# Row and column tiles of the array, and fewer but longer DVE instructions, in the state-space core of a decoder

## The chip, the cores and the metric

The program runs on one core of a Trainium2 chip. The metric is the device time of one execution in microseconds (us). Of the kernel before there are three timed runs: 1267.12, 1269.05 and 1270.66 us, median 1269.05 us.

## The reference, cut to what matters

The reference is a two-layer decoder on 512 tokens of 1024 channels. Layer 0 has a state-space mixer and a feed-forward part, layer 1 has attention and a feed-forward part. The change is in the mixer alone:

```
u = h @ w_in                                # 64 groups of 16 channels
bu = einsum('gnk,lgk->lgn', b, u)           # b complex: 64 states per group
x_l = a * x_(l-1) + bu_l                    # a complex and diagonal, scan over l
y = Re(einsum('gkn,lgn->lgk', c, x)) + d * u
z = gelu(y); val, gate = split(z @ w_glu); out = val * sigmoid(gate)
```

## The kernel before, in words

The 512 tokens are 128 chunks (C) of four places (T). The 64 groups are 32 pairs; eight channel tiles (NCT) take four pairs (PPC) each. A pair has 2 x 64 states, which fill the 128 partitions, and 2 x 16 channels. All operands of this core are float32.

`s5_core` first splits the input and the weights into two parts for the input projection (`project`, eight halves of 48 products of 256 columns, written here as lines L141 to L143), and works out powers of the transition (L315 to L386). Then each tile t goes through these steps:

- `coefs` (L437): the input weights `W` and output weights `E` for the four places, by products and sums on DVE and POOL (`g` is POOL). ACT copies `W` into the buffers `Wbd` and `W0`, and `spread` copies `E` into `Obd`: with zeros around them, so that the two groups of a pair stand in a block-diagonal operand of 128 rows.
- `rotor` (L498): cosine and sine of the chunk's rotation, `Cs` and `Sn`: four products on DVE, two sums on POOL.
- `taps` (L524, PE lines L532 and L535): the products within a chunk, evacuated by ACT into `Tb`.
- `turn_w` and `turn_u` (L547, L557): transposes of the input weights and of u.
- `scan` (L562): PE makes the chunk inputs V (L569), DVE rotates them (four products), POOL adds (`ra`, `rc`), DVE runs the recurrence over the 128 chunks (L581, eight scans of 128), rotates back (four products), and POOL adds the states `Xr`, `Xi`.
- `outputs` (L597 to L599): three products per pair, then GELU on ACT (L601).
- `turn_y` (L609): transposes back, and a split into two parts (`zh` on ACT, `zl` on DVE L157).
- `partial` (L623): each finished tile goes at once into the first output tiles of the gated unit (12 products of 512 columns).

The rest of the gated unit, the feed-forward parts and the attention follow. They are long runs of products of 512 columns, for which DVE and ACT split each weight slab (`wh`, `wl`, L129 and L130).

The order on every engine is set when the program is built: a scheduler moves the instructions by a cost model of its own (`TCARGS`). Each engine then works off its list in order, and waits on semaphores. Buffers with a name and `bufs=n` rotate over n places; four PSUM banks (`x`) rotate over all uses of the tile steps.

## Time and profile before

| | |
|---|---|
| timed runs, median | 1269.05 us |
| profiled execution: span, first to last instruction | 1265.5 us (the page gives no other time of it) |
| mixer core (first instruction to the last transposes of tile 7) | 0 to 229 us |
| rest of the gated unit, up to the first row sums of the feed-forward part | 229 to 310.6 us |
| PE, DVE, ACT and POOL busy in 0 to 229 us | 184.0, 203.8, 118.0, 151.8 us |

How to read it: PE is TensorE's products, DVE is VectorE, ACT ScalarE, POOL GpSimd. After 229 us PE has hardly a pause until the end of the program. Up to there every engine waits for some other in turn. The clock column is the share of TensorE's full clock that was granted: 1.00 is 2.4 GHz, 0.50 is 1.2 GHz. A PE row's duration overlaps the next one's: a row "x8" of 1.06 us whose single members last 0.275 us has its members (1.06 - 0.275) / 7 = 0.112 us apart. A float32 product stands as two records, a transpose as one.

### The profile page before, as it was taken

The page shows a single profiled execution, that of the slowest core. Times are in us where ns is not written, and L with a number is a line of the kernel's source. Part 1 is how long each engine was busy: PE and PEld are TensorE (multiplying, and loading weights), DVE is VectorE, ACT ScalarE, POOL GpSimd, SP SyncE. Part 2 cuts the span into 40 slices and gives each one's busy share as a digit, 9 for nine tenths or more (in the row PEclk, how much of TensorE's full clock was granted, in tenths as well). Part 3 has the DMA queues.
Part 4 walks back from the last instruction along what each step waited for, and adds up shares of the span by engine and source line. Part 5 has one row for each costly group of instructions (what it writes and reads, how often), then busy time and mean ns, then how long its engine had stood idle before and what let it go on. Part 6 is the DMA issues. An engine that isn't in the chain of part 4 may idle for free.

```text
span 1265.5 us, 15056 instructions
## 1 busy us (share of the span) xinstructions
PE 1207.8 (95%) x5808; PEld 1000.6 (79%) x5808; DVE 707.2 (56%) x1241; ACT 482.8 (38%) x815; POOL 276.6 (22%) x248
## 2 busy tenths in 40 slices
PE   5987878999999999999999899999999999999998
PEld 4987767788888888888878677777888888888887
DVE  9999988335744444433336877754664444443221
ACT  5475443324433322322224666653433223332210
POOL 4777765003000000000042544342200000000000
PEclk9997778999999999999999999999999999999999
DMA  4210001333223332333322111101333332223431
GB/s 158 80 30 21 18 9 37 97 100 99 95 92 99 100 100 91 94 103 92 94 82 81 36 36 41 50 1 51 100 100 100 100 100 92 93 95 100 118 121 49
DMA packets 31895, 99.82 MB, mean 79 GB/s; under 512 B 3664, under 2 KB 5712, under 8 KB 31824
## 3 DMA queue, kind: packets, MB, share of 16 engines
q1 hardware_dynamic: 31680, 98.86, 25.2%
q8 instruction: 45, 0.74, 0.2%
q14 instruction: 26, 0.21, 0.1%
q10 hardware_dynamic: 144, 0.00, 0.0%
HBM read 96.75 MB, written 2.10 MB: 78 GB/s over the span
## 4 chain that ended last, share of the span: by engine, by line
PE 78%; DVE 3%; ACT 1%; issue 0%; DMA 0%; POOL 0%; DVEq 0%; ACTq 0%
PE ps_ps L141 19%; PE ps_ps L142 19%; PE ps_ps L143 19%; PE ps_s L922 3%; PE ps_po L959 2%; PE ps_a L141 2%; PE ps_a L143 2%; PE ps_a L142 2%; PE ps_x L141 2%; PE ps_x L143 2%; PE ps_x L142 2%; PE ps_a L939 1%; PE ps_a L907 1%; DVE wl L130 1%; ACT wh L129 1%
## 5 line engine op out<-in xcount | busy, mean ns | idle before, releaser
L129 ACT ACTIVATE wh<-w 128x1024 fp32r<-128x1024 f32 (+3 forms) x193 | 190.7, 992 | 534.3 <-PE ps_ps L142 337.1
L130 DVE TENSOR_TENSOR wl<-w,wh 128x1024 fp32r<-128x1024 f32 (+3 forms) x193 | 230.7, 1197 | 201.6 <-ACT wh L129 201.5
L141 PE MATMUL ps_ps<-fh,wh 128*128 128x512 f32 x704 | 274.2, 390 | 0.0
L143 PE MATMUL ps_ps<-fh,wl 128*128 128x512 f32 x704 | 273.4, 389 | 0.0
L142 PE MATMUL ps_ps<-fl,wh 128*128 128x512 f32 x704 | 273.4, 389 | 0.0
L141 PEld LDWEIGHTS ps_ps<-fh,wh 128*128 128x128 f32 x704 | 132.2, 188 | 27.9 <-issue 0.5
L142 PEld LDWEIGHTS ps_ps<-fl,wh 128*128 128x128 f32 x704 | 132.2, 188 | 27.7 <-issue 0.5
L143 PEld LDWEIGHTS ps_ps<-fh,wl 128*128 128x128 f32 x704 | 132.2, 188 | 27.5
L141 PE MATMUL ps_ps<-ah,wh 128*128 128x512 f32 x352 | 136.9, 389 | 0.0
L142 PE MATMUL ps_ps<-al,wh 128*128 128x512 f32 x352 | 136.9, 389 | 0.0
L143 PE MATMUL ps_ps<-ah,wl 128*128 128x512 f32 x352 | 136.9, 389 | 0.0
L249 POOL TENSOR_TENSOR acc<-acc,sq 128x512 f32<-128x512 f32 x21 | 31.4, 1495 | 423.3 <-ACT sq L248 422.8
L698 DVE TENSOR_TENSOR ut<-ps_ps,rstd 128x512 f32<-128x512 f32 x44 | 30.4, 691 | 127.8 <-PE ps_ps L143 127.8
L143 PEld LDWEIGHTS ps_ps<-ah,wl 128*128 128x128 f32 x352 | 66.1, 188 | 13.8
L695 DVE TENSOR_TENSOR gt<-ps_ps,rstd 128x512 f32<-128x512 f32 x44 | 30.4, 691 | 83.2 <-PE ps_ps L143 83.1
L142 PEld LDWEIGHTS ps_ps<-al,wh 128*128 128x128 f32 x352 | 66.1, 188 | 13.7
L141 PEld LDWEIGHTS ps_ps<-ah,wh 128*128 128x128 f32 x352 | 66.1, 188 | 13.6
L930 POOL TENSOR_SCALAR p<-p,sm 128x128 f32<-128x128 f32 (+2 forms) x48 | 45.3, 948 | 64.4 <-DVE sm L928 54.2
L922 PE MATMUL ps_s<-kT,qT 96*128 96x256 f32 (+3 forms) x128 | 44.9, 454 | 1.8 <-ACT kT L909 1.0
L925 DVE TENSOR_REDUCE mx<-ps_s 128x1 f32<-128x128 f32 (+3 forms) x64 | 30.7, 487 | 22.2 <-PE ps_s L923 21.5
L927 ACT ACTIVATE p<-ps_s,mx 128x128 f32<-128x128 f32 (+3 forms) x64 | 33.3, 524 | 21.9 <-DVE mx L925 18.8
L156 ACT ACTIVATE ah<-ut 128x512 fp32r<-128x512 f32 x44 | 27.9, 633 | 30.8 <-DVE ut L699 30.8
(391 smaller groups left out, 2081.0 us busy)
## 6 DMA issues: line engine op xcount, KB each, us to landing
...
```

Source lines behind the costliest of these rows:

```text
L129: nc.scalar.activation(out=wh[:, c], in_=w[:, c], func=AF.Copy)
L130: nc.vector.tensor_tensor(out=wl[:, c], in0=w[:, c], in1=wh[:, c].bitcast(F32), op=ALU.subtract)
L141: nc.tensor.matmul(out=out, lhsT=lh, rhs=rh, start=start, stop=False)
L142: nc.tensor.matmul(out=out, lhsT=lh, rhs=rl, start=False, stop=False)
L143: nc.tensor.matmul(out=out, lhsT=ll, rhs=rh, start=False, stop=stop)
L249: nc.gpsimd.tensor_tensor(out=acc, in0=acc, in1=sq, op=ALU.add)
L695: v.tensor_tensor(out=gt, in0=pss[0], in1=rstd, op=ALU.mult)
L698: v.tensor_tensor(out=ut, in0=pss[1], in1=rstd, op=ALU.mult)
L922: nc.tensor.matmul(out=ps, lhsT=qT[:, i * P:n], rhs=kT[:, 0:n], start=True, stop=False)
L925: v.reduce_max(out=m1, in_=ps, axis=AX.X, negate=True)
L927: nc.scalar.activation(out=pb, in_=ps, func=AF.Exp, bias=m1, accum_out=s1)
L930: eng.tensor_scalar(out=pb, in0=pb, scalar1=s1, scalar2=None, op0=M_)
```

## The change

- The operands of 128 rows with zeros go (`Wbd`, `W0`, `Obd`). The products read one group at a time from 64 of the 128 rows, and write to 64 of the 128 columns where the output has 64 rows. `taps` becomes 32 products of 64 rows by 64 columns and two of 64 rows (two banks instead of one), `scan` 16 products of 64 by 64 with 128 moving columns (8 of 128 by 128 before), `outputs` four full products and 16 of 64 rows (12 full ones before). `turn_w` has four transposes instead of eight.
- `coefs` works out `W` and `E` for both real parts in three DVE instructions each, of 512 and of 640 elements; nothing of it is left on POOL. The signed copies of the powers that this needs (`ArS`, `AiN`, `GrS`, `GiS`) are made once, by eight ACT instructions.
- In `scan`, both sums of the rotations move from POOL to DVE, the eight scans of 128 become two of 512 (`RH` holds the decay, with a zero at each pair's first chunk, which ACT fills per tile), and the back rotation becomes two products of 1016.
- `rotor` has eight DVE products of 256 instead of four of 512; its two sums stay on POOL. Its `t1`, `t2` share the single buffers `pc`, `qc` with the scan's products.

```
-            sqs.append(cp.tile([P, S], F32, name="xsq", tag=("ra", "rb", "rc", "rd")[k % 4]))
+            if k % 2 == 0:
+                two = cp.tile([P, 2, S], F32, name="xsq", tag=("z", "z", "pc", "qc")[k // 2], bufs=2 if k < 4 else 1)
+            sqs.append(two[:, k % 2])
...
+        ArS, AiN, GrS, GiS = (sp.tile([P, NCT * 2, 2, 2 * n], F32, name=m) for m, n in (("ArS", T + 1), ("AiN", T + 1), ("GrS", T), ("GiS", T)))
+        for o, x, n, signs in ((ArS, Ar, T + 1, (1.0, -1.0)), (AiN, Ai, T + 1, (-1.0, -1.0)), (GrS, Gr, T, (1.0, 1.0)), (GiS, Gi, T, (-1.0, 1.0))):
+            for c in range(2):
+                nc.scalar.activation(out=o[:, :, c], in_=x.rearrange("p (a e) j -> p a (e j)", e=2), func=AF.Copy, scale=signs[c])
...
-        Wbd = [sp.tile([P, PPC, 2, T, 2, 16], F32, name=f"Wbd{i}") for i in range(NB)]
-        W0 = [sp.tile([P, PPC, 2, T, 2, 16], F32, name=f"W0{i}") for i in range(NB)]
-        Obd = [sp.tile([P, PPC, 2, T, 2, 16], F32, name=f"Obd{i}") for i in range(NB)]
-        Tb = [sp.tile([P, PPC, T, 2, 16], F32, name=f"Tb{i}") for i in range(3)]
-        Xr = [sp.tile([P, PPC, C], F32, name=f"Xr{i}") for i in range(NB)]
-        Xi = [sp.tile([P, PPC, C], F32, name=f"Xi{i}") for i in range(NB)]
+        Wz = [sp.tile([P, 2 * PPC, 5, 16], F32, name=f"Wz{i}") for i in range(NB)]
+        Tb = [sp.tile([P, 2, 2, 2, T, 16], F32, name=f"Tb{i}") for i in range(3)]
+        X = [sp.tile([P, 2, PPC, C], F32, name=f"X{i}") for i in range(NB)]
+        RH = [sp.tile([P, PPC, C], F32, name=f"RH{i}") for i in range(NB)]
...
+            g.memset(Wz[b], 0.0)
+            g.memset(X[b][:, :, :, 0:1], 0.0)
+            g.memset(RH[b][:, :, 0:1], 0.0)
...
+            def weigh(o, j, n, re, im):
+                def bb(x):
+                    return x.unsqueeze(2).broadcast_to([P, 2 * PPC, n, 16])
+
+                def gg(x):
+                    return x[:, 2 * t:2 * t + 2].rearrange("p a c (e j) -> p (a c e) j", e=2).unsqueeze(3).broadcast_to([P, 2 * PPC, n, 16])
+
+                ma, mb = (cp.tile([P, 2 * PPC, n, 16], F32, name="w" + z, tag="e" + z, bufs=1) for z in "ab")
+                tt(ma, bb(bc[:, j]), gg(re), M_)
+                tt(mb, bb(bc[:, j + 1]), gg(im), M_)
+                tt(o, ma, mb, A_)
+
+            W = cp.tile([P, 2 * PPC, T, 16], F32, name="W")
+            weigh(W, 0, T, GrS, GiS)
+            nc.scalar.activation(out=Wz[t % NB][:, :, 1:5:2], in_=W[:, :, 0:1, :].broadcast_to([P, 2 * PPC, 2, 16]), func=AF.Copy)
+            E = cp.tile([P, 2 * PPC, T + 1, 16], F32, name="E", bufs=3)
+            weigh(E, 2, T + 1, ArS, AiN)
+            coef[t] = {"E": E, "W": W}
...
+            t1 = cp.tile([P, PPC, C], F32, name="t1", tag="pc", bufs=1)
+            t2 = cp.tile([P, PPC, C], F32, name="t2", tag="qc", bufs=1)
...
             for o, x, y in ((Cs, bcs, bcs), (t1, bsn, bsn), (Sn, bsn, bcs), (t2, bcs, bsn)):
-                tt(o.rearrange("p a (b c) -> p a b c", b=8), lo16(x), hi16(y), M_)
+                for e in range(2):
+                    tt(o[:, 2 * e:2 * e + 2].rearrange("p a (b c) -> p a b c", b=8), pairs(x, e)[:, :, 0:16].unsqueeze(2).broadcast_to([P, 2, 8, 16]),
+                       pairs(y, e)[:, :, 16:24].unsqueeze(3).broadcast_to([P, 2, 8, 16]), M_)
             tt(Cs, Cs, t1, S_, g)
             tt(Sn, Sn, t2, A_, g)
...
+        def taps(t):
+
+
+            b = t % NB
+            E = coef[t]["E"]
+            kps = [self.ps("x") for _ in range(2)]
+            for odd in (1, 0):
+                for q in range(2):
+                    for c in range(2):
+                        for e in range(2):
+                            for g2 in range(2):
+                                h = slice(64 * g2, 64 * g2 + 64)
+                                r = 4 * q + 2 * c + e
+                                wz = Wz[b][h, r, (0 if odd else 1):(4 if odd else 5)]
+                                nc.tensor.matmul(out=kps[g2][64 * e:64 * e + 64, 64 * q + (0 if odd else 16):64 * q + 64],
+                                                 lhsT=wz.rearrange("p i k -> p (i k)"),
+                                                 rhs=E[h, r, 0:(T if odd else T - 1)].rearrange("p a b -> p (a b)"),
+                                                 start=odd == 1 and q == 0 and c == 0, stop=odd == 0 and c == 1, skip_group_check=True)
             for g2 in range(2):
                 h = slice(64 * g2, 64 * g2 + 64)
-                for c in range(2):
-                    nc.scalar.activation(out=Obd[t % NB][h, :, c, :, g2, :], in_=coef[t]["E"][h, :, c, 1:, :], func=AF.Copy)
-
...
-            for i in range(T):
-                r = slice(32 * i, 32 * i + 32)
-                for g2 in range(2):
-                    nc.scalar.activation(out=Tb[t % 3][r, :, T - 1 - i:, g2, :], in_=k4[r, :, 0:i + 1, :], func=AF.Copy,
-                                         scale=self.c("g2mask")[r, g2:g2 + 1])
+                nc.tensor.matmul(out=kps[g2][:, 0:128].rearrange("p (a u k) -> p a u k", a=2, u=T)[:, :, 0:2, :], lhsT=self.c("places")[h],
+                                 rhs=DI[h, 2 * t:2 * t + 2].rearrange("p a (u k) -> p a u k", u=2), start=False, stop=True, skip_group_check=True)
+            for g2 in range(2):
+                k4 = kps[g2][:, 0:128].rearrange("p (a u k) -> p a u k", a=2, u=T)
...
+            ps_w = self.ps("x")
+            W = coef[t]["W"].rearrange("p (a e) i k -> p a (e i k)", e=2)
+            for r in range(4):
+                nc.tensor.transpose(out=ps_w[:, r * P:(r + 1) * P], in_=W[:, r], identity=ident)
+            WT = cp.tile([P, 2, 2, P], F32, name="WT")
+            nc.scalar.activation(out=WT.rearrange("p a b c -> p (a b c)"), in_=ps_w, func=AF.Copy)
...
         def scan(t):
+
...
-            V = []
+            nc.scalar.activation(out=RH[b][:, :, 1:].rearrange("p (e a) c -> p e a c", e=2),
+                                 in_=rho[:, t * PPC:(t + 1) * PPC].rearrange("p (a e) -> p e a", e=2).unsqueeze(3).broadcast_to([P, 2, 2, C - 1]), func=AF.Copy)
+            ps_v = [self.ps("x") for _ in range(2)]
+            for q in range(2):
+                for c in range(2):
+                    for g2 in range(2):
+                        for e in range(2):
+                            h = slice(64 * e, 64 * e + 64)
+                            nc.tensor.matmul(out=ps_v[e][64 * g2:64 * g2 + 64, (2 * q + c) * C:(2 * q + c + 1) * C],
+                                             lhsT=WT[h, q, c, 64 * g2:64 * g2 + 64], rhs=uT[h, q, g2], start=True, stop=True)
+            pc, qc = (cp.tile([P, 2, PPC, C], F32, name=n, bufs=1) for n in ("pc", "qc"))
+            for e in range(2):
+                vv = ps_v[e].rearrange("p (a c k) -> p c a k", a=2, c=2)
+                for o, w in ((pc, Cs), (qc, Sn)):
+                    tt(o[:, :, 2 * e:2 * e + 2], vv, w[:, 2 * e:2 * e + 2].unsqueeze(1).broadcast_to([P, 2, 2, C]), M_)
+            z = cp.tile([P, 2, PPC, C], F32, name="z")
+            tt(z[:, 0], pc[:, 0], qc[:, 1], A_)
+            tt(z[:, 1], pc[:, 1], qc[:, 0], S_)
             for c in range(2):
...
-            tt(ra, V[0], Cs, M_)
-            tt(rd, V[0], Sn, M_)
-            tt(rb, V[1], Sn, M_)
-            tt(rc, V[1], Cs, M_)
-            tt(ra, ra, rb, A_, g)
-            tt(rc, rc, rd, S_, g)
-            for z in (ra, rc):
-                for pp in range(PPC):
-                    rj = rho[:, t * PPC + pp:t * PPC + pp + 1].broadcast_to([P, C])
-                    v.tensor_tensor_scan(out=z[:, pp], data0=rj, data1=z[:, pp], initial=0.0, op0=M_, op1=A_)
+                v.tensor_tensor_scan(out=z[:, c].rearrange("p a b -> p (a b)"), data0=RH[b].rearrange("p a b -> p (a b)"),
+                                     data1=z[:, c].rearrange("p a b -> p (a b)"), initial=0.0, op0=M_, op1=A_)
...
-            tt(xr, ra[:, :, :n], Cs[:, :, :n], M_)
-            tt(xi, ra[:, :, :n], Sn[:, :, :n], M_)
-            tt(rb[:, :, :n], rc[:, :, :n], Sn[:, :, :n], M_)
-            tt(rd[:, :, :n], rc[:, :, :n], Cs[:, :, :n], M_)
-            tt(xr, xr, rb[:, :, :n], S_, g)
-            tt(xi, xi, rd[:, :, :n], A_, g)
+            xc, xs = (cp.tile([P, 2, PPC, C], F32, name="x" + m, tag=m, bufs=1) for m in ("pc", "qc"))
+            for o, w in ((xc, Cs), (xs, Sn)):
+                tt(o[:, :, :, :n], z[:, :, :, :n], w[:, :, :n].unsqueeze(1).broadcast_to([P, 2, PPC, n]), M_)
+            tt(X[b][:, 0, :, 1:], xc[:, 0, :, :n], xs[:, 1, :, :n], S_)
+            tt(X[b][:, 1, :, 1:], xc[:, 1, :, :n], xs[:, 0, :, :n], A_)
 
...
+            uT, E = states[t], coef[t]["E"]
+            ps_y = [self.ps("x") for _ in range(2)]
+            for g2 in range(2):
+                for q in range(2):
+                    nc.tensor.matmul(out=ps_y[g2][:, 128 * q:128 * q + 128], lhsT=uT[:, q, g2], rhs=Tb[t % 3][:, q, g2].rearrange("p e j k -> p (e j k)"),
+                                     start=q == 0, stop=False, skip_group_check=True)
+            for q in range(2):
+                for e in range(2):
+                    for c in range(2):
+                        for g2 in range(2):
+                            h = slice(64 * g2, 64 * g2 + 64)
+                            nc.tensor.matmul(out=ps_y[g2][:, 128 * q + 64 * e:128 * q + 64 * e + 64], lhsT=X[b][h, c, 2 * e + q],
+                                             rhs=E[h, 4 * q + 2 * c + e, 1:].rearrange("p j k -> p (j k)"),
+                                             start=False, stop=c == 1, skip_group_check=True)
+            Y = cp.tile([P, T, PPC, 2, 16], F32, name="Y", bufs=1)
+            for g2 in range(2):
+                nc.scalar.activation(out=Y.rearrange("p j a b k -> p a j b k")[:, :, :, g2], in_=ps_y[g2][:, 0:256].rearrange("p (a j k) -> p a j k", a=PPC, j=T),
+                                     func=AF.Gelu_apprx_tanh)
...
         for t in range(NCT):
             for f, d in ((turn_u, 1), (later_u, 0), (rotor, 1), (scan, 1), (turn_w, 2), (later_p, 6), (outputs, 0),
-                         (taps, 2), (later_p, 7), (partial, -1), (turn_y, 0), (spread, 2), (coefs, 3)):
+                         (taps, 2), (later_p, 7), (partial, -1), (turn_y, 0), (coefs, 3)):
```

On PE, the first tile's steps, from its transposes of u (`ps_x<-ctab,U`) through the taps (`E` with the input weights `W` or `Wz`, and the skip weights `DI`) to the transposes of the weights. Before:

```order
L557 MATMUL ps_x<-ctab,U 128x128 x4
L532 MATMUL ps_x<-E,W_308 128x64
L535 MATMUL ps_x<-DI,ctab 128x16
L532 MATMUL ps_x<-E,W_308 128x64 x2
L535 MATMUL ps_x<-DI,ctab 128x16
L532 MATMUL ps_x<-E,W_308 128x64 x2
L535 MATMUL ps_x<-DI,ctab 128x16
L532 MATMUL ps_x<-E,W_308 128x64 x2
L535 MATMUL ps_x<-DI,ctab 128x16
L532 MATMUL ps_x<-E,W_308 128x64
L547 MATMUL ps_x<-ctab,Wbd_306 128x128 x8
```

And now:

```order
L544 MATMUL ps_x<-ctab,U 128x128 x4
L514 MATMUL ps_x<-E,Wz_314 64x64 x16
L514 MATMUL ps_x<-E,Wz_314 64x48 x16
L520 MATMUL ps_x<-DI,ctab 128x2x32 x2
L534 MATMUL ps_x<-ctab,W 128x128 x4
```

The skip weights no longer stand between the taps, the taps are 32 narrower products instead of eight, and the weight transposes are four instead of eight.

On DVE, the scan of tile 1 and what stands beside it (`ra`, `rc` are its two parts, `Xr`, `Xi` the states, `E` an output weight, `Cs`, `Sn` the rotor). Before, from its recurrence on:

```order
L581 SCALAR_TENSOR_TENSOR ra<-dr,ra 128x128 x4
L581 SCALAR_TENSOR_TENSOR rc<-dr,rc 128x128 x4
L320 TENSOR_TENSOR Xr_316<-ra,Cs 128x4x127
L320 TENSOR_TENSOR Xi_318<-ra,Sn 128x4x127
L320 TENSOR_TENSOR rb<-rc,Sn 128x4x127
L320 TENSOR_TENSOR rd<-rc,Cs 128x4x127
L320 TENSOR_TENSOR E<-ea,eb 128x4x80
L476 SCALAR_TENSOR_TENSOR E<-ea,eb 128x4x80
L320 TENSOR_TENSOR Sn<-bsn,bcs 128x512
L320 TENSOR_TENSOR ra<-ps_x,Cs 128x512
L320 TENSOR_TENSOR rd<-ps_x,Sn 128x512
```

And now, from the rotor on that this scan uses (`t` its products, `pc`, `qc` the products from PSUM, `z` both parts, `xpc`, `xqc` the back rotation):

```order
L322 TENSOR_TENSOR Cs<-bcs 128x256 x2
L322 TENSOR_TENSOR X_319<-xpc,xqc 128x4x127 x2
L322 TENSOR_TENSOR Sn<-bsn,bcs 128x256 x2
L322 TENSOR_TENSOR t_924<-bsn 128x256 x2
L322 TENSOR_TENSOR t_925<-bcs,bsn 128x256 x2
L322 TENSOR_TENSOR pc<-ps_x,Cs 128x2x256 x2
L322 TENSOR_TENSOR qc<-ps_x,Sn 128x2x256 x2
L322 TENSOR_TENSOR z<-pc,qc 128x512 x2
L571 SCALAR_TENSOR_TENSOR z<-RH_322,z 128x512 x2
L322 TENSOR_TENSOR xpc<-z,Cs 128x8x127
```

Eight short scans are two long ones, the sums into `z` stand here, and `pc` comes straight behind the rotor's `t`, whose buffer it takes.

On POOL, the stretch that serves one tile. Before (`wb`, `W`, `eb` belong to the weights, `ra`, `rc`, `Xr`, `Xi` to the scan, `Cs`, `Sn` to the rotor):

```order
L320 TENSOR_TENSOR Cs<-Cs,t_1190 128x512
L320 TENSOR_TENSOR ra<-ra,rb 128x512
L320 TENSOR_TENSOR rc<-rc,rd 128x512
L320 TENSOR_TENSOR Sn<-Sn,t_1191 128x512
L320 TENSOR_TENSOR Xr_316<-Xr_316,rb 128x4x127
L320 TENSOR_TENSOR Xi_318<-Xi_318,rd 128x4x127
L320 TENSOR_TENSOR wb<-bc,Gi 128x256 x2
L320 TENSOR_TENSOR Cs<-Cs,t_1354 128x512
L320 TENSOR_TENSOR W<-wa,wb 128x4x64 x2
L320 TENSOR_TENSOR ra<-ra,rb 128x512
L320 TENSOR_TENSOR rc<-rc,rd 128x512
```

And now, from the last step of the powers (`Gi`) on:

```order
L322 TENSOR_TENSOR Gi<-mm 128x128
L322 TENSOR_TENSOR Cs<-Cs,t_671 128x512
L322 TENSOR_TENSOR Sn<-Sn,t_672 128x512
L322 TENSOR_TENSOR Cs<-Cs,t_924 128x512
L322 TENSOR_TENSOR Sn<-Sn,t_925 128x512
```

Only the two rotor sums of each tile are left on POOL.

## Rows read from the trace of the kernel before

**Rows 1.** The page: busy time by engine and its share of the span.

```profile
PE 1207.8 (95%) x5808; PEld 1000.6 (79%) x5808; DVE 707.2 (56%) x1241; ACT 482.8 (38%) x815; POOL 276.6 (22%) x248
```

**Rows 2.** Busy time of each engine by stage, granted clock (PEclk), DMA share.

```profile
28.00:90.00 62.00, 61.56 (x473) 60.50 (x472) 59.33 (x115) 36.87 (x75) 45.94 (x46) 0.97 0.18 56
90.00:100.00 10.00, 0.97 (x5) 0.78 (x4) 10.00 (x12) 2.41 (x4) 6.74 (x7) 0.74 0.05 13
100.00:205.00 105.00, 88.57 (x505) 79.96 (x504) 96.86 (x146) 52.98 (x118) 75.39 (x53) 0.80 0.06 18
229.00:311.00 82.00, 81.22 (x356) 66.48 (x356) 36.37 (x41) 31.48 (x42) 9.64 (x7) 1.00 0.32 98
72.67:217.61 144.94, 117.95 (x720) 106.80 (x718) 133.53 (x198) 73.24 (x157) 100.17 (x74) 0.84 0.08 22
```

**Rows 3.** Groups of DVE by form, 72 to 218 us.

```profile
L581 DVE TENSOR_TENSOR_SCAN ra<-dr,ra 128x128 f32<-128x128 f32 x32 | 26.4, 881 | 1.4 <-POOL ra L320 1.4
L581 DVE TENSOR_TENSOR_SCAN rc<-dr,rc 128x128 f32<-128x128 f32 x32 | 11.2, 412 | 0.0
...
L320 DVE TENSOR_TENSOR rb<-ps_x,Sn 128x512 f32<-128x512 f32 x8 | 5.4, 681 | 2.1 <-PE ps_x L569 2.1
```

**Rows 4.** Groups of POOL by form, 72 to 218 us.

```profile
L320 POOL TENSOR_TENSOR Sn<-Sn,t 128x512 f32<-128x512 f32 x7 | 10.5, 1505 | 5.9 <-DVE t L320 5.9
...
L320 POOL TENSOR_TENSOR Cs<-Cs,t 128x512 f32<-128x512 f32 x7 | 9.4, 1341 | 2.8 <-DVE t L320 2.8
```

**Rows 5.** DVE in order of time: start, length, instruction, count, idle before.

```profile
110.34 0.68 DVE L320 TENSOR_TENSOR rd<-rc,Cs 128x508 f32<-128x508 f32 x1
110.93 0.48 DVE L320 TENSOR_TENSOR E<-ea,eb 128x320 f32<-128x320 f32 x1
...
131.26 0.42 DVE L320 TENSOR_TENSOR wa<-bc,Gr 128x256 f32<-128x256 f32 x1
131.59 0.49 DVE L476 SCALAR_TENSOR_TENSOR E<-ea,eb 128x320 f32<-128x320 f32 x1
```

**Rows 6.** DVE, the first product of tile 0 and the last of tile 7.

```profile
72.67 0.69 DVE L320 TENSOR_TENSOR ra<-ps_x,Cs 128x512 f32<-128x512 f32 x1
...
216.93 0.68 DVE L320 TENSOR_TENSOR rd<-rc,Cs 128x508 f32<-128x508 f32 x1
```

**Rows 7.** PE in order of time: taps (L532, L535), projection, inputs of a scan.

```profile
121.54 0.39 PE L535 MATMUL ps_x<-DI,ctab 32*128 32x16 f32 x2
121.86 0.66 PE L532 MATMUL ps_x<-E,W 128*128 128x64 f32 x4
122.45 0.39 PE L535 MATMUL ps_x<-DI,ctab 32*128 32x16 f32 x2
...
125.31 0.39 PE L142 MATMUL ps_g<-zl,wh 128*128 128x512 f32 x1
125.54 0.39 PE L143 MATMUL ps_g<-zh,wl 128*128 128x512 f32 x1
125.99 1.16 PE L569 MATMUL ps_x<-uT,WT 128*128 128x128 f32 x8
```

**Rows 8.** Durations of one product (ns, min/median/max), 128 rows and 32 rows.

```profile
L569 PE MATMUL ps_x<-uT,WT x128: 270/275/421, 71.6 to 207.8; 128*128 128x128 f32 x128
...
L801 PE MATMUL ps_s<-ctab,krraw x4: 221/222/243, 688.4 to 688.6; 32*128 32x32 f32 x4
```

**Rows 9.** PE, four transposes of 32 rows, in a later stage.

```profile
688.35 0.43 PE L801 MATMUL ps_s<-ctab,krraw 32*128 32x32 f32 x4
```

**Rows 10.** PE at the first outputs.

```profile
89.59 0.60 PE L557 MATMUL ps_x<-ctab,U 128*128 128x128 f32 x4
99.23 0.80 PE L597 MATMUL ps_x<-Tb,uT 128*128 128x128 f32 x2 [9.03 <-DVE rd L320]
```

**Rows 11.** PE, the last transposes of the core.

```profile
228.38 0.60 PE L609 MATMUL ps_x<-ctab,Y 128*128 128x128 f32 x4
```

**Rows 12.** The chain that ended last, where the feed-forward takes its first row sums.

```profile
310.58 0.86 PE ps_ps L689 x2
```

More of the change, by code (lines that the diff above doesn't have):

```diff
@@ new lines, in taps @@
+            for g2 in range(2):
[5 more added lines that the diff above has]
+                for e in range(2):
+                    for ip in range(2):
+                        h = slice(64 * e + 32 * ip, 64 * e + 32 * ip + 32)
+                        n = 2 * ip + 2
+                        nc.scalar.activation(out=Tb[t % 3][h, :, g2, e, T - n:, :], in_=k4[h, :, 0:n, :], func=AF.Copy)
@@ L555, in turn_u @@
             ps_u = self.ps("x")
-            for pp in range(PPC):
-                nc.tensor.transpose(out=ps_u[:, pp * C:(pp + 1) * C],
-                                    in_=Us[t // 2][:, (t % 2) * PPC + pp].rearrange("p a b c -> p (a b c)"), identity=ident)
-            nc.scalar.activation(out=uT.rearrange("p a b -> p (a b)"), in_=ps_u, func=AF.Copy)
+            U = Us[t // 2].rearrange("p (a e) i k -> p a (e i k)", e=2)
+            for r in range(4):
+                nc.tensor.transpose(out=ps_u[:, r * C:(r + 1) * C], in_=U[:, 4 * (t % 2) + r], identity=ident)
@@ L560, in turn_u @@
+            nc.scalar.activation(out=uT.rearrange("p a b c -> p (a b c)"), in_=ps_u, func=AF.Copy)
             states[t] = uT
@@ L564, in scan @@
             Sn, Cs, WT, uT = coef[t]["Sn"], coef[t]["Cs"], coef[t]["WT"], states[t]
-            V = []
-            for c in range(2):
-                ps_v = self.ps("x")
-                for pp in range(PPC):
-                    nc.tensor.matmul(out=ps_v[:, pp * C:(pp + 1) * C], lhsT=WT[c][:, pp], rhs=uT[:, pp], start=True, stop=True)
-                V.append(ps_v.rearrange("p (a b) -> p a b", a=PPC))
-            ra, rb, rc, rd = (cp.tile([P, PPC, C], F32, name=n) for n in ("ra", "rb", "rc", "rd"))
@@ L591, in outputs @@
+            tt(X[b][:, 0, :, 1:], xc[:, 0, :, :n], xs[:, 1, :, :n], S_)
+            tt(X[b][:, 1, :, 1:], xc[:, 1, :, :n], xs[:, 0, :, :n], A_)
         def outputs(t):
             b = t % NB
-            uT = states[t]
-            ps_y = self.ps("x")
-            for pp in range(PPC):
-                o = ps_y[:, pp * P:(pp + 1) * P]
-                nc.tensor.matmul(out=o, lhsT=uT[:, pp], rhs=Tb[t % 3][:, pp].rearrange("p a b c -> p (a b c)"), start=True, stop=False)
-                nc.tensor.matmul(out=o, lhsT=Xr[b][:, pp], rhs=Obd[b][:, pp, 0].rearrange("p a b c -> p (a b c)"), start=False, stop=False)
-                nc.tensor.matmul(out=o, lhsT=Xi[b][:, pp], rhs=Obd[b][:, pp, 1].rearrange("p a b c -> p (a b c)"), start=False, stop=True)
@@ L603, in outputs @@
+            Y = cp.tile([P, T, PPC, 2, 16], F32, name="Y", bufs=1)
+            for g2 in range(2):
+                nc.scalar.activation(out=Y.rearrange("p j a b k -> p a j b k")[:, :, :, g2], in_=ps_y[g2][:, 0:256].rearrange("p (a j k) -> p a j k", a=PPC, j=T),
+                                     func=AF.Gelu_apprx_tanh)
             states[t] = Y
```

108 lines of the change are left out of this document (22 added, 86 removed).

## The prediction, made before the changed kernel ran

> **What bounds the kernel now.** I read the page first: PE is busy 1207.8 of the span of 1265.5 us [rows 1], so nearly all of its 58 idle us must lie somewhere, and only a stage where PE waits can give time. The table by stage [rows 2] says where. From 28 to 90 us PE is busy 61.56 of 62 us at a granted clock of 0.97: saturated by the input projection. From 90 to 100 it works 0.97 of 10 us. From 100 to 205 it works 88.57 of 105 us at a granted clock of 0.80, while DVE works 96.86. From 229 on it is dense again (81.22 of 82 at 1.00), up to the first row sums of the feed-forward part at 310.58 [rows 12]. So the core is bounded by PE up to 90 us, by DVE from its first rotation product to its last, and by PE behind that.
>
> The first outputs show the handover: PE ends the transposes of u at about 90.2 and stands 9.03 us for DVE's `rd` [rows 10]. DVE's stretch runs from 72.67 to 217.61 (216.93 and 0.68) [rows 6], 144.94 us, of which it is busy 133.53 and idle 11.41 [rows 2].
>
> How much of the 133.53 is work? Where POOL is quiet, DVE instructions start 0.59 us apart after 508 elements and 0.33 after 256 [rows 5]. That is 0.066 us for each instruction and 1.03 ns for each element: 0.60 for 512, 0.40 for 320, 0.73 for 640, 1.12 for 1016 or 1024. The scans of `rc` take 11.2 us for 32, or 0.35 each; those of `ra`, the same instruction while POOL still adds, 881 ns in the mean against 412 [rows 3]. The order has 197 DVE instructions in this stretch: 72 of 512 (43.2), 32 of 508 (18.9), 20 of 320 (8.0), 8 of 256 (2.6), one of 1024 (1.1), 64 scans (22.4). Sum 96.3 us. So 37.2 us of DVE's busy time are disturbance, while POOL is busy 100.17 us [rows 2]: 0.37 us lost for each us of POOL.
>
> **The change part by part.** I follow DVE through the same stretch, then add what stands ahead of it and behind it.
>
> *DVE's own work.* The order now has 189 instructions from the first product of tile 0 to the last sum into `X` of tile 7: 73 of 512 (43.8), 52 of 256 (17.2), 15 of 640 (11.0), 16 of 508 (9.4), 17 of 1016 or 1024 (19.0) and 16 scans of 512. No scan of 512 is in the trace. At most it costs four of 128 (1.40), at least a product of 512 (0.60); the row it is nearest to is the scan, less three times the fixed 0.066, so I take 1.20, 19.2 in all. Sum 119.6 us: 23.3 more than now. The merging saves little; the sums taken over from POOL cost 16 x 0.60 + 16 x 0.59 = 19.0, and the coefficients about 1.7 more for each of five tiles.
>
> *Disturbance.* Of some sixteen POOL instructions per tile two remain, 14 in the stretch; `Sn` takes 1505 ns in the mean and `Cs` 1341 [rows 4], so 7 x 2.85 = 19.9 us of POOL. At 0.37 this costs 7.4 us. The bounds are nothing, and their full length, 19.9. I take 7.4 since the operations and their neighbours are the same as now. The Trainium skill, SBUF — State Buffer, section Who interferes with whom, says that a DVE instruction with two inputs in SBUF and a POOL instruction that reads SBUF lock each other out for a whole instruction. The slow scans of `ra` bear the lock out; by its letter the 14 sums could cost 19.9 and not 7.4, and that is a rival below.
>
> *Waits.* Of DVE's 11.4 idle us the waits for POOL's sums and for free buffers go. The wait for PE's inputs of the scan stays, 2.1 us in `rb`'s group [rows 3]. One is new: `t1` and `t2` share single buffers with the scan's `pc` and `qc`, so the first product of a scan waits until POOL has read `t1` and `t2`. In five of seven tiles the order has other work between; in two, as in tile 1, `pc` stands right behind the last rotor product `t`, and of POOL's sum behind that (1.5) I give it 0.8, the half. Behind the waiting `pc` stands the whole scan and, on PE, that tile's outputs. So 2.1 + 1.6 = 3.7 us; bounds nothing and 11.4. DVE's stretch becomes 119.6 + 7.4 + 3.7 = 130.7 us against 144.94.
>
> *The start.* DVE's first product waits for PE, which is saturated there, so each added PE record counts. The order puts 6 more projection products ahead of the first scan (0.7 us at 0.12, half of the 0.23 that 512 columns take [rows 7]). It puts 46 more records of the taps there: 35 narrow products and two for places, two records each, against 12, less four transposes. And all 32 records of the scan must be done where the first 8 sufficed. A narrow record is not in the trace. Eight full ones take 1.16 us with 0.275 for the last, so 0.126 apart there; the four of 32 rows and 32 columns take 0.43 with 0.222, so 0.07 apart [rows 7 to 9]. I take 0.07, the row nearest in size, and keep a quarter of that and 0.126 as ends. Taps 46 x 0.07 = 3.2 (0.8 to 5.8), scan 32 x 0.07 - 8 x 0.126 = 1.2 (nothing to 3.0). First product at 72.67 + 0.7 + 3.2 + 1.2 = 77.8; between 74 and 82. The Trainium skill, TensorE: Matmul & The Clock Gate, Part 3 (Packing small matmuls), says that products in different row groups run together, which these pairs could do. No row of this kernel shows it; by it a record would count about half and the start fall by 2.2 us, which is inside my bounds.
>
> *Around it.* The signed copies (eight ACT instructions, once) and the longer way from POOL's last power `Gi` over ACT to DVE lie beside the projection, where PE is the bound; if that cover were gone, they would cost about 2 us. ACT works 52.98 of 105 us [rows 2] and loses the copies into `Wbd`, `W0`, `Obd`: it is no bound.
>
> *The end.* DVE ends at 77.8 + 130.7 = 208.5 instead of 217.61, and POOL's last `Xr`, `Xi`, which came behind, are gone. Then the order has the last 32 records and products of outputs(7) (2.7), 20 products of the gated unit at 0.23 (4.6, GELU beside them), `turn_y` (0.7) and 366 more products before the first row sums, where before it has 353 (228.38 + 0.7 + 353 x 0.231 = 310.6 checks with [rows 11, 12]). 366 x 0.231 = 84.5. Row sums at 208.5 + 2.7 + 4.6 + 0.7 + 84.5 = 301.0 against 310.58: 9.6 us earlier. PE is dense behind that, so it is passed on whole. The profiled span of 1265.5 becomes 1255.9. The median of the timed runs is 3.5 above this span (the page gives no other time), so the median 1269.05 becomes 1259.5, rounded to 1260.
>
> **Does PE keep up?** Per tile it gets 128 narrow records (9.0 at 0.07), 12 full ones (1.5), 12 transposes (1.3), 12 products of 512 columns (2.8), and about ten changes between narrow and full operands. Such a change costs: from one `L535` pair to the next, 121.54 to 122.45, lie four full records and two narrow ones, 4 x 0.126 + 2 x 0.07 = 0.64 of 0.91, so about 0.13 for each of two [rows 7]. Sum 15.9 us at full clock. DVE needs for a middle tile coefficients 4.0, rotor 2.7, scan and rotations 9.4, parts of slabs and of the output 1.2, together 17.3, and with disturbance 1.1 and waits 0.5 it is 18.9. So DVE stays the bound, but at the granted clock of 0.80 of this stretch PE would need 19.9: the margin is thin.
>
> **The rivals.**
> - *PE and DVE wait for each other.* At a clock of 0.80 PE loses 1.0 us on DVE in each of five middle tiles, and with both lists in order I put 4 more us of waits to it: 9 in all, 1269. For it: 0.80 now [rows 2], and PE works as much as before. Against: where PE has no gaps, the clock is 0.97 to 1.00.
> - *The narrow records cost as much as full ones* (0.126, no running together). PE's tile becomes 128 x 0.126 + 6.9 = 23.0 us, 4.1 above DVE in each of five tiles: 20.5; the start moves 4.4, outputs(7) 1.8. That is 26.7 - 9.6 = 17 us slower, 1286; at 0.10 PE's tile is 19.7, the loss 0.8 x 5 + 2.3 + 0.9 = 7.2, and little is won. It decides from about 0.10 us a record at full clock, from some 0.085 at 0.85. For it: the taps of 64 columns now stand 0.66 for four, about 0.13 apart, no cheaper than 128 columns [rows 7], so the load of operands and not the columns may set the pace. Against: the four of 32 rows at 0.07. A middle case, 0.113, gives 2.5 x 5 + 3.4 + 1.4 - 9.6 = 7.7, 1277.
> - *POOL's sums block DVE for their whole length*, by the lock above: 19.9 instead of 7.4, 12.5 more, 1272. Against it: 0.37 in this trace.
> - *Hardly any disturbance is left.* Two sums per tile fall into DVE's instructions from PSUM or its waits: 7.4 and some 2 us of start go, 1250.
>
> **How the numbers follow.** Forecast 0.45, own range 1254 to 1265; both wait 0.20; narrow records dear 0.17; whole lock 0.05; hardly any disturbance 0.13. The smallest difference that a measurement of this kernel can tell is 0.3%, 3.8 us, so faster is below 1265.2. Faster: 0.43 + 0.13 + 0.02 of the second = 0.58. Slower is above 1272.9: 0.15 of the third, 0.05 of the second, 0.02 of the fourth: 0.22. The rest, 0.20, is no change. The range goes from 1250, the last rival, to 1278, just above the middle case of the dear records; beyond it lie about 0.08 below and 0.11 above.
>
> **What the profile after would show.** Narrow records 0.07 apart within a row "x32" (wrong: over 0.1). First `pc` from PSUM at 77.8, last `X` at about 208.5, first row sums at 301. DVE in that stretch some 127 us busy of 131, scans of 512 at 1.2, POOL near 20 us. If PE between 100 and 200 us has no gaps and DVE idles for `ps_x`, PE has become the bound. If `pc` waits for POOL in more than two tiles, the shared buffers cost more than I gave them.

## The result, and the profile after

The changed kernel takes 1252.26 us (median of four runs, 1250.36 to 1255.63) against 1268.09 us of the kernel before on the same chips: ratio 0.988, 95% interval 0.9863 to 0.9897, 15.8 us faster. Forecast were 1260 us, about 9 faster. The profiled execution has a span of 1250.3 us. One execution further below, of ten with the narrow products in another order, was over 1.5% longer than the shortest of its kernel, and the ratio there leaves it out.

The stages of the changed kernel, with the columns of [rows 2], and the stretch of DVE in the last row:

```profile
28.00:90.00 62.00, 57.79 (x594) 55.90 (x592) 60.18 (x124) 28.40 (x70) 16.03 (x17) 0.89 0.21 65
90.00:100.00 10.00, 9.53 (x85) 8.60 (x83) 9.40 (x17) 3.75 (x10) 1.32 (x1) 0.82 0.09 28
100.00:205.00 105.00, 91.72 (x932) 77.66 (x932) 95.61 (x144) 32.93 (x86) 19.56 (x11) 0.84 0.08 24
220.00:300.00 80.00, 80.00 (x352) 65.88 (x351) 37.00 (x43) 30.50 (x40) 9.64 (x7) 1.00 0.31 99
67.91:204.22 136.31, 118.44 (x1194) 102.19 (x1186) 125.05 (x191) 45.90 (x119) 23.82 (x14) 0.82 0.07 23
```

PE no longer stands still from 90 to 100 us (9.53 busy, before 0.97). DVE's stretch from its first rotation product to its last lasts 136.31 us instead of 144.94. POOL is busy 23.82 us in it instead of 100.17.

DVE in order of time at the places that answer to [rows 6], and the new waits:

```profile
67.91 0.68 DVE L322 TENSOR_TENSOR pc<-ps_x,Cs 128x512 f32<-128x512 f32 x1
...
81.40 0.75 DVE L322 TENSOR_TENSOR t<-bcs,bsn 128x256 f32<-128x256 f32 x2
83.30 1.29 DVE L322 TENSOR_TENSOR pc<-ps_x,Cs 128x512 f32<-128x512 f32 x2 [1.16 <-POOL Cs L322]
...
194.46 0.69 DVE L322 TENSOR_TENSOR pc<-ps_x,Cs 128x512 f32<-128x512 f32 x1 [5.78 <-PE ps_x L560]
...
202.94 1.29 DVE L322 TENSOR_TENSOR X<-xpc,xqc 128x508 f32<-128x508 f32 x2
```

The first product comes at 67.91 (before 72.67), the last sum into `X` ends at 204.2 (before 217.61). `pc` waits for POOL's rotor sum, and once, before the last tile, 5.78 us for PE. The groups of DVE and of POOL, as [rows 3, 4]:

```profile
L571 DVE TENSOR_TENSOR_SCAN z<-RH,z 128x512 f32<-128x512 f32 x16 | 18.8, 1208 | 0.0
L322 DVE TENSOR_TENSOR qc<-ps_x,Sn 128x512 f32<-128x512 f32 x16 | 10.5, 682 | 0.8 <-POOL Sn L322 0.8
L322 DVE TENSOR_TENSOR pc<-ps_x,Cs 128x512 f32<-128x512 f32 x16 | 10.5, 682 | 9.3 <-PE ps_x L560 5.8 <-POOL Cs L322 3.5
```

```profile
L322 POOL TENSOR_TENSOR Cs<-Cs,t 128x512 f32<-128x512 f32 x7 | 13.9, 1983 | 113.0 <-DVE t L322 113.0
L322 POOL TENSOR_TENSOR Sn<-Sn,t 128x512 f32<-128x512 f32 x7 | 10.1, 1444 | 1.6 <-DVE t L322 1.6
```

A scan of 512 takes 1.21 us. PE in order of time, as [rows 7]: taps and places of the first tile, then scan, outputs and taps of a middle tile:

```profile
61.38 1.15 PE L514 MATMUL ps_x<-E,Wz 64*64 64x64 f32 x64
62.45 0.44 PE L520 MATMUL ps_x<-DI,ctab 64*128 64x64 f32 x4
...
100.04 1.10 PE L560 MATMUL ps_x<-uT,WT 64*64 64x128 f32 x32
101.07 0.71 PE L587 MATMUL ps_x<-Tb,uT 128*128 128x128 f32 x4
101.71 2.00 PE L594 MATMUL ps_x<-E,X 64*128 64x64 f32 x16
...
105.15 1.14 PE L514 MATMUL ps_x<-E,Wz 64*64 64x64 f32 x32
```

The 64 records of the first tile's taps last 1.15 us, so they start 0.017 us apart; the 32 of a scan 0.03 apart; but the 16 of one half of the outputs 0.12. The chain reaches the first row sums at 295.86, before at 310.58 [rows 12]:

```profile
295.86 0.86 PE ps_ps L685 x2
```

| us | before | forecast | after |
|---|---|---|---|
| DVE's first product | 72.67 | 77.8 | 67.91 |
| DVE's stretch | 144.9 | 130.7 | 136.3 |
| from there to the row sums | 93.0 | 92.5 | 91.6 |
| row sums | 310.58 | 301.0 | 295.86 |

So 14.7 us are won up to the row sums: 4.8 by an earlier start, 8.6 in DVE's stretch, 1.3 behind it. The 8.6 are DVE's busy time, 133.53 before and 125.05 now; it is idle as long as before, 11.4 and 11.3 us.

### The profile page after: what moved, and what is told of

Read it like the earlier page. It is cut to its first block, busy times and chain, and to the rows that moved or that the text cites. A ratio compares the mean times of both kernels' runs of the same rounds, so it can differ in the third digit from the quotient of the medians.

```text
span 1250.3 us, 16034 instructions
## 1 busy us (share of the span) xinstructions
PE 1206.1 (96%) x6384; PEld 994.5 (80%) x6384; DVE 693.7 (55%) x1241; ACT 450.9 (36%) x775; POOL 173.0 (14%) x164
## 4 chain that ended last, share of the span: by engine, by line
PE 79%; DVE 2%; ACT 1%; DMA 0%; POOL 0%; issue 0%; DVEq 0%
PE ps_ps L142 19%; PE ps_ps L141 19%; PE ps_ps L143 19%; PE ps_s L918 3%; PE ps_po L955 2%; PE ps_a L141 2%; PE ps_a L143 2%; PE ps_a L142 2%; PE ps_x L143 2%; PE ps_x L142 2%; PE ps_x L141 2%; PE ps_a L935 1%; PE ps_a L903 1%; PE ps_s L141 0%; PE ps_s L143 0%; PE ps_s L142 0%
## 5 line engine op out<-in xcount | busy, mean ns | idle before, releaser
L130 DVE TENSOR_TENSOR wl<-w,wh 128x1024 fp32r<-128x1024 f32 (+3 forms) x193 | 224.8, 1167 | 197.4 <-ACT wh L129 197.2
L594 PE MATMUL ps_x<-E,X 64*128 64x64 f32 x256 | 36.3, 310 | 5.2 <-DVE X L322 5.1
```

The lines of the kernel that those rows point to most:

```text
L130: nc.vector.tensor_tensor(out=wl[:, c], in0=w[:, c], in1=wh[:, c].bitcast(F32), op=ALU.subtract)
L594: nc.tensor.matmul(out=ps_y[g2][:, 128 * q + 64 * e:128 * q + 64 * e + 64], lhsT=X[b][h, c, 2 * e + q], rhs=E[h, 4 * q + 2 * c + e, 1:].re ...
```

## The experiments

All ratios are to the kernel before, which ran on the same chip each time; where two edited kernels are compared with each other, they ran at other times, and differences under some 4 us say little. Every edit deals the whole order out anew, so a run shows its edit and that. Each kernel has one profiled execution.

**DVE's half alone**, in the kernel before:

```diff
-            tt(ra, ra, rb, A_, g)                       # and rc, xr, xi
+            tt(z[:, 0], pc[:, 0], qc[:, 1], A_)         # all four on DVE
-                    v.tensor_tensor_scan(out=z[:, pp], ...)   # 8 of 128
+                v.tensor_tensor_scan(out=z[:, c].rearrange("p a b -> p (a b)"), ...)   # 2 of 512
```

> The kernel before with only DVE's half of scan changed: sums of both rotations on DVE, two scans of 512, back rotation in two products of 1016; operands of PE, coefficients (partly on POOL), and zeroed buffers as before. Theory: most of the 8.7 us that DVE's stretch gained comes from taking POOL's sums away, PE's tiles only keep PE out of the way: DVE's work 96 + 8 x 2.1 = 113 us, POOL still busy some 55 us there at 0.37 lost per us, idle 8: 141 down to about 137 to 142 us against 144.9, and no sums of POOL behind it; start as before (72.7): 1258 to 1264 us. Rival: without the narrow products PE holds DVE back, and nothing is won: 1266 to 1272. Other rival: the narrow products do nothing for the time, all comes from DVE: 1252 to 1256.

1252.92 us, ratio 0.9881 (0.9867 to 0.9896): the whole gain, with none of the narrow products. Its stretch, columns as above:

```profile
77.22:206.31 129.09, 109.92 (x736) 99.32 (x734) 124.23 (x167) 74.34 (x159) 48.52 (x41) 0.92 0.09 26
```

It is 129.1 us, shorter than the 136.3 of the whole change, at a granted clock of 0.92 and with PE busy 109.9. Against the kernel before DVE is busy 9.3 us less and idle 6.6 less. The gain is smaller than that, since the first product comes at 77.2; PE lost 3.63 us in the projection to a late slab:

```profile
56.89 0.58 PE L142 MATMUL ps_g<-wl,sh 128*128 128x256 f32 x1 [3.63 <-DVE wl L130]
```

**The sums alone**, in the kernel before:

```diff
-            tt(ra, ra, rb, A_, g)
+            tt(ra, ra, rb, A_)          # and so for rc, xr, xi
```

> The kernel before with one thing changed: the four sums of scan's rotations on DVE instead of POOL. Eight scans, four products back, two buffers each, and all of PE as before. Theory: of DVE's half the move of the sums away from POOL is the main part and the merging the smaller: DVE gets 19.0 us of work, POOL loses 55 us of its 100 in the stretch, at 0.37 this gives 20 back, the waits for POOL's sums and the states that POOL finished behind DVE go; with merging the whole half is worth 15, and the merged instructions are worth 8 x 0.5 = 4 by price: 1255 to 1260 us. Rival: a sum costs DVE as much as it saves (19 against 20), the merging makes the gain: 1264 to 1270 us.

1259.94 us, ratio 0.9938 (0.9924 to 0.9951), in the theory's range: 8.7 of the 15 us.

```profile
72.62:211.03 138.41, 119.51 (x720) 105.91 (x718) 133.00 (x228) 71.35 (x154) 54.27 (x42) 0.85 0.07 24
```

30 of the 32 sums lie in this stretch, 17.9 us of priced work more for DVE, and it is busy 133.0 us, hardly changed from 133.53, while POOL fell from 100.17 to 54.27. So the sums cost DVE in busy time what they give back, as the rival had it. What is won in the stretch, 6.5 us, is idle time: 5.4 us where there were 11.4. POOL with fewer sums delivers the input weights `W` in time. DVE's waits for them, in the stretch before and in this one (releaser, us in total, times, longest):

```profile
DVE ea L320 <- POOL W L320: 5.4, 3, 2.4
...
DVE ea L320 <- POOL W L320: 0.6, 1, 0.6
```

The merging is worth the other 7.0 us: with it DVE is busy 124.23 us in the run above, 8.8 less than here, where the price of the merged instructions had 4.

**PE's half alone**, in the changed kernel:

```diff
-            tt(z[:, 0], pc[:, 0], qc[:, 1], A_)
+            tt(z[:, 0], pc[:, 0], qc[:, 1], A_, g)      # all four on POOL; 8 scans of 128; 4 products of 508
```

> The counterpart of the run with DVE's half alone: the changed kernel (narrow products, coefficients on DVE) with DVE's part of scan as in the kernel before: the four sums of the rotations on POOL, eight scans of 128, the back rotation in four products of 508. The products stay in single buffers, of which the kernel before had two. Theory: the gain is DVE's half, the narrow products by themselves bring nothing (the run with DVE's half alone needs as long as the whole change): DVE's work 119.6 - 19.0 + 4 = 105 us, POOL some 61 us at 0.37 lost per us, waits for the sums: stretch 140 to 150 us, 1262 to 1270 us. Rival: the narrow products are worth as much as DVE's half, either alone gets most of it: 1252 to 1257.

1274.8 us, ratio 1.0065 (1.0041 to 1.009): slower than before, and slower than the theory had it. DVE's waits show why it is no clean counterpart: with single buffers for the products DVE stands for POOL's sums.

```profile
DVE t L322 <- POOL X L322: 14.8, 7, 2.4
DVE z L572 <- POOL z L322: 10.1, 7, 1.5
```

So this run can't say what the narrow products bring alone: how much of the loss is theirs and how much the single buffers' stays open. That they add nothing to DVE's half is shown by the run with DVE's half alone.

**Order of the narrow products**, in the changed kernel:

```diff
-            for odd in (1, 0): ... for e in range(2): for g2 in range(2):    # taps
+            for e in range(2): for g2 in range(2): for odd in (1, 0): ...
-            for q in range(2): for c in range(2): for g2 in range(2): for e in range(2):    # scan
+            for e in range(2): for g2 in range(2): for q in range(2): for c in range(2):
```

> The changed kernel with the products of taps and of scan in another order: four to eight that stand in a row read the same 64 rows and write the same 64 columns, instead of changing rows and columns from one to the next. Same products, same sizes. Theory: products of different quarters of the array run beside each other, so four quarters share the time of one; in one quarter the records of taps will stand about 0.07 us apart (4 x 0.017), those of scan about 0.13 (4 x 0.032), PE gets some 5 us more per tile and becomes the bound: 1265 to 1285 us against 1252. Rival: a narrow record is short by its size alone, the order doesn't matter: 0.017 and 0.032 stay, 1252.

Median 1279.89 us of ten runs (they scatter from 1268 to 1293), ratio 1.0071 (1.0044 to 1.0099), in the theory's range.

```profile
61.54 3.35 PE L514 MATMUL ps_x<-E,Wz 64*64 64x64 f32 x64
...
106.61 2.56 PE L560 MATMUL ps_x<-uT,WT 64*64 64x128 f32 x32
```

The same 64 records of taps now take 3.35 us instead of 1.15, the 32 of scan 2.56 instead of 1.10, all four at a granted clock of 1.00. Size alone does not make them quick; neighbours in different quarters of the array do. The middle tiles of the changed kernel lie between: there the taps of one row half stand together and only the columns change, and 32 records take 1.14 us. In all these products the other row half is also another PSUM bank, so rows and banks are not told apart. The spacing (0.05 and 0.07) is below the 0.07 and 0.13 that I had put for one quarter. PE becomes the bound, busy 159.48 of 163.22 us, and its granted clock is only 0.70:

```profile
70.79:234.01 163.22, 159.48 (x1204) 141.05 (x1201) 125.23 (x189) 43.89 (x117) 23.54 (x14) 0.70 0.06 19
```

**Full outputs**, in the changed kernel:

```diff
+            nc.scalar.activation(out=Obd[t % NB][h, :, :, g2, :], in_=coef[t]["E"][h, :, 1:, :], func=AF.Copy)
-                            nc.tensor.matmul(..., lhsT=X[b][h, c, 2 * e + q], rhs=E[h, 4 * q + 2 * c + e, 1:]...)   # 16 of 64 rows
+                        nc.tensor.matmul(..., lhsT=X[b][:, c, 2 * e + q], rhs=Obd[b][:, 4 * q + 2 * c + e]...)      # 8 of 128
```

> The changed kernel with outputs as full products again: ACT spreads the output weights into a buffer with zeros around (two copies per tile), PE makes eight products of 128 rows by 128 columns and four of the taps into one bank, one GELU instead of two. taps and scan stay narrow. In the changed kernel the narrow records of outputs stand 0.12 us apart, as far as full ones, since all of one bank read the same 64 rows; they are 32 in place of 16. Theory: PE saves 5.1 - 2.4 = 2.7 us per tile, the wait for the last scan's inputs (5.8 us) goes: 1246 to 1250 us. Rival: DVE is the bound throughout and PE's time is hidden, or the zeroing of the two buffers at the start (1.8 us of POOL) takes it back: 1251 to 1255.

1242.4 us (1241.93 to 1242.71), ratio 0.9798 (0.9779 to 0.9818): 10 us faster than the changed kernel, 25.6 than the kernel before, more than expected.

```profile
188.22 1.72 PE L599 MATMUL ps_x<-Obd,X 128*128 128x128 f32 x14
```

```profile
68.17:199.11 130.94, 104.63 (x1065) 89.04 (x1064) 123.89 (x192) 51.17 (x124) 25.44 (x14) 0.86 0.09 28
```

Full records stand 0.11 us apart, about as the half ones did, and there are half as many. PE is busy 104.6 us in the stretch instead of 118.4. DVE's stretch falls by 5.4 to 130.9, with the 5.78 us wait gone, and what is left behind it by 6 to 85.7 us, since PE has done more of the gated unit by then (380 records are left there, where the changed kernel has 419). This version beats both, and it keeps the narrow taps and scan. DVE's half without them, and with the coefficients partly on POOL, took 1252.92; so with full outputs the rest of the change is worth some 10 us, without them nothing.

**Rotor sums on DVE**, in the changed kernel (`g` left out of both sums):

> The changed kernel with the rotor's two sums on DVE too, so that POOL has nothing left to do beside DVE's stretch. DVE gets 14 x 0.60 = 8.4 us more work and loses about 5 us of disturbance and 4.3 us of waits. Theory (a sum on POOL costs DVE by disturbance and wait about as much as the sum itself): 1250 to 1253 us. Rival (POOL's remaining sums are nearly free, DVE's own work counts in full): 1256 to 1260. In its trace no DVE instruction of the stretch should be longer than its undisturbed length if POOL is what disturbs.

1256.37 us, ratio 0.9907 (0.989 to 0.9925): the rival's time, but not by its reason.

```profile
68.99:204.54 135.55, 122.66 (x1174) 104.90 (x1166) 128.56 (x205) 45.02 (x118) 0.00 (x0) 0.76 0.08 23
```

With POOL at 0.00 DVE is busy 128.56 us for 128 of priced work: undisturbed, and the stretch is 0.7 us shorter than the changed kernel's. So DVE's busy time rose by 3.5 us for 8.4 us of work, as the theory had it, and POOL is what disturbs. The loss lies behind the stretch, 96.0 us to the row sums instead of 91.6. The changed kernel and this one, from the stretch's end to the row sums:

```profile
204.22:295.86 91.64, 91.58 (x419) 75.88 (x420) 38.39 (x44) 33.30 (x44) 9.64 (x7) 0.98 0.28 92
204.54:300.54 96.00, 96.00 (x430) 79.61 (x430) 38.48 (x43) 33.90 (x45) 9.64 (x7) 0.95 0.28 88
```

PE has 11 records more left there, and works them at a granted clock of 0.95 instead of 0.98; the clock makes about 3 of the 4.4 us (an estimate: 96.0 x 0.95 is 91.2, 91.6 x 0.98 is 89.8). Why it was lower the run does not show. The intervals of the two ratios overlap a little (the changed kernel has 0.9863 to 0.9897).

**Own buffers for the rotor**, in the changed kernel (`tag="t1"`, `tag="t2"` in place of `pc`, `qc`):

> The changed kernel with two buffers of their own for the rotor's products t1 and t2 (they share those of pc and qc otherwise). Theory: DVE sets the end of the stretch, so the waits of pc and qc for POOL's sums of the rotor (3.5 and 0.8 us in the trace) go, and the time falls by up to 4: 1248 to 1250 us. Rival: PE's inputs for the last scan, for which DVE stands 5.8 us, set it: DVE only waits longer there, 1251 to 1254.

1257.34 us, ratio 0.9916 (0.9896 to 0.9936): some 5 us slower than the changed kernel, against both, though the intervals just touch. The waits for POOL are gone and the stretch is 1 us shorter, but the new order puts 18 more projection products ahead of the first scan, and the first product comes 4.7 us later:

```profile
72.59 0.68 DVE L322 TENSOR_TENSOR pc<-ps_x,Cs 128x512 f32<-128x512 f32 x1
```

**Late zeroing**, in the kernel before (the zeroing of `Wbd`, `Obd`, `W0`, `Tb` after a copy of the sums of squares):

> The kernel before, with the zeroing of the block-diagonal buffers and of the taps' buffers by POOL moved from the start of the program to about 18 us, where POOL has nothing to do (each waits for one small copy of the sums of squares). Theory: at the start this zeroing holds DVE's second rounding step (4.16 us instead of 0.25) and with it all of DVE's splits, so the changed kernel, whose buffers are smaller, gains about 4 us there: this step will take 0.25 us, the row sums of the input come 3 to 4 us earlier on PE, DVE's first rotation product at 69 instead of 72.7, 1264 to 1265 us against 1268. Rival: the earlier start of the changed kernel comes from its narrower taps and its order alone: no change, 1268.

1273.7 us, ratio 1.0048 (1.0036 to 1.006): slower, against both. The step at the start, in the kernel before:

```profile
3.64 4.16 DVE L179 TENSOR_SCALAR en<-ex 128x32 f32<-128x32 f32 x1
```

In this run, DVE, POOL and PE:

```profile
3.01 0.18 DVE L179 TENSOR_SCALAR en<-ex 128x32 f32<-128x32 f32 x1
...
19.41 7.03 DVE L179 TENSOR_SCALAR dn<-dx 128x64 f32<-128x64 f32 x1
...
19.66 6.79 DVE L130 TENSOR_TENSOR wl<-w,wh 128x1024 fp32r<-128x1024 f32 x1
20.81 5.66 DVE L180 TENSOR_SCALAR tn<-tn 128x32 f32<-128x32 f32 x1
```

```profile
20.99 0.94 POOL L631 MEMSET Wbd<- 128x1024 f32 x1
...
25.45 0.94 POOL L633 MEMSET W<- 128x1024 f32 x1
```

```profile
26.55 0.80 PE L142 MATMUL ps_x<-wl,sh 128*128 128x256 f32 x2 [8.43 <-DVE tn L180]
```

The step at the start now takes 0.18 us instead of 4.16. But the DVE instructions that begin from 19.41 to 20.81 all end at about 26.45, just as POOL has zeroed six buffers in a row, 20.99 to 26.39. One of them is the split `wl`, 6.79 us long, and PE stands 8.43 us until it is there. The first product comes at 76.95, 4.3 later than before. So the cost moved with the zeroing. Three zeroings of 512 columns behind it, 26.35 to 27.91, held nothing for long.

**More zeroing**, in the changed kernel (`X` and `RH` whole, 1536 columns more):

> The changed kernel with more zeroing by POOL at its start: the whole of the states' and the decay's buffers instead of their first column, and 1536 columns of a buffer that nothing reads; about 3.9 us more, so that it ends near 7.5 us as in the kernel before. Theory (zeroing holds DVE): DVE's rounding step takes about 4 us, everything behind comes 3 to 4 us later, 1255 to 1257 us against 1252. Rival (start by taps and order): 1252.

1260.52 us, ratio 0.993 (0.9915 to 0.9945), some 8 us above the changed kernel's median. The profiled execution is the shortest of its six (1255.91): first product at 69.08, 1.2 later, row sums 3 later. What makes the others longer it does not show. POOL zeroes without a pause until 7.63 us, but DVE's second step is not held 4 us:

```profile
2.86 0.85 DVE L190 TENSOR_SCALAR ex<-smalls 128x32 f32<-128x32 f32 x1 [1.98 <-DMA smalls<-smalls]
3.75 0.46 DVE L179 TENSOR_SCALAR en<-ex 128x32 f32<-128x32 f32 x1
4.25 0.57 DVE L180 TENSOR_SCALAR en<-en 128x32 f32<-128x32 f32 x1
```

Each of these steps ends as one zeroing ends (3.68, 4.17, 4.78), not as the last does. And the zeroing of the kernel before does not always hold the step for 4 us either. The runs with DVE's half alone and with the sums alone zero as much at the start, and there the same step, also at 3.64, takes less:

```profile
3.64 1.83 DVE L179 TENSOR_SCALAR en<-ex 128x32 f32<-128x32 f32 x1
...
3.64 0.93 DVE L179 TENSOR_SCALAR en<-ex 128x32 f32<-128x32 f32 x1
```

| us | zeroing ends | step `en` lasts | 200th product of the projection starts |
|---|---|---|---|
| before | 7.77 | 4.16 | 52.43 |
| DVE's half alone | 7.89 | 1.83 | 50.83 |
| sums alone | 7.87 | 0.93 | 50.16 |
| more zeroing | 7.63 | 0.46 | 49.65 |
| changed kernel | 3.58 | 0.25 | 49.27 |

PE's lead at the 200th product goes with the length of the hold and not with the end of the zeroing. With the old zeroing it lies between 0.9 and 3.2 us behind the changed kernel. How much of the 3.2 us the change brings, and how much is this one execution of the kernel before, stays open; what makes a hold long too.

**Rotor written earlier**, in the version with full outputs:

```diff
-            ... (rotor, 1), (scan, 1), ...
+            ... (scan, 1), (rotor, 2), ...
```

> The changed kernel with full outputs (1242.4 us), with the rotor of a tile written behind the scan of the tile before, ahead of the coefficients, so that coefficients stand on DVE between the rotor's products and the scan that needs POOL's sums of them. Theory: the waits of pc and qc for POOL (5.9 + 0.8 us there) go, DVE sets the end: 1237 to 1241 us. Rival: another wait takes their place (GELU and split of the tile before, the inputs of the scan): 1241 to 1246 us.

1242.62 us, ratio 0.9799 (0.9785 to 0.9812). The order on DVE came out the same but for the names of the buffers, and the waits with it (5.8 us where there were 5.9). So it tells nothing of the waits:

```profile
DVE pc L322 <- POOL Cs L322: 5.9, 5, 1.2
```

This row is of the version with full outputs before that edit. Whether these waits can go stays open.

## Why the prediction was right, and where it was not

- **DVE is the bound, and POOL's sums are worth moving: held.** DVE got 23.3 us more priced work, and its busy time fell by 8.5 us, from 133.53 to 125.05. The sums alone show the exchange: 17.9 us more work, no more busy time. What they gained is 6.0 us of idle time, the waits for POOL that I had going away; in the whole change other waits took their place.
- **Disturbance 7.4: measured 5.4**, or 0.23 for each us of POOL. The rival of the whole lock (19.9) is out for these sums. That POOL is what disturbs is shown by the rotor's sums on DVE: with POOL idle 128.56 us are busy for 128.0 priced.
- **Scan of 512 at 1.20: 1.21.**
- **Waits 3.7: measured 11.3.** 4.3 of it are the waits for POOL's sums, in four tiles and not two (3.5 of `pc`, 0.8 of `qc`). The large one, 5.78, was in the rival of PE and DVE waiting for each other: PE came late with the last scan.
- **The start: wrong in size and sign**, 77.8 against 67.91. The step that failed is the term "Taps 46 x 0.07 = 3.2". A record of the new taps takes 0.017, the lower bound; and the old ones, which I took off at 0.07 too, took 0.15 (0.91 for six [rows 7]). So 1.5 us of taps and places stand for 3.6, four transposes less save 0.4, the scan costs 0.1 more: 2.1 + 0.4 - 0.1 = 2.4 us saved where I had 4.4 to pay, 6.8 of the 9.9. The rest is outside that step: I left the splits of the input as they were, but the 200th product of the projection starts at 49.27 instead of 52.43 us, 3.2 earlier. How much of that is the change's own stays open, by the table of the zeroing runs.
- **That 1252 lies in the range is in part luck.** The start was 9.9 us too late in my sum, DVE's stretch 5.6 too short (136.3 against 130.7), what stands behind it 0.9 too long. Two errors of opposite sign leave 5.1 at the row sums, 295.86 against 301.0.
- **Narrow products together.** The order experiment shows a factor of 2.3 to 2.9 between neighbours in different quarters and neighbours in one. The Trainium skill, TensorE: Matmul & The Clock Gate, Part 3 (Packing small matmuls), says that products in different row groups run together. The trace agrees, and what I had kept inside the bounds decides here. The outputs show the limit: each half reads one half of the rows, and its records are as far apart as full ones. Only in the last tile, where the scheduler mixed the halves, do 28 records take 1.78 us, 0.06 apart:

```profile
203.68 0.44 PE L594 MATMUL ps_x<-E,X 64*128 64x64 f32 x4 [2.67 <-DVE X L322]
204.28 1.78 PE L594 MATMUL ps_x<-E,X 64*128 64x64 f32 x28 [0.16 <-DVE X L322]
```

- **PE per tile: 15.9 forecast.** By the rows above a tile has 64 taps (1.1 to 2.2), scan 1.0, outputs 5.2, four places (0.4 to 0.7), 12 transposes 1.3 and 2.8 of the gated unit: 12 to 13 us at full clock. But taps and scan save what outputs add: PE is busy 118.44 us in DVE's stretch, before 117.95. That is why PE's half added nothing; with full outputs PE is busy 104.6 and the time falls by 10 us.
- **The rival of dear records** fell for taps and scan and held for outputs. **The rival of hardly any disturbance** forecast 1250 and is nearest to the time, but by other terms.
- **Against the rival of mutual waiting I wrote that the clock is 0.97 to 1.00 where PE has no gaps. That failed:** in the order experiment PE is busy 98% of the stretch at 0.70.
